# S5's state products: 64 table columns in one product, read at a stride of eight elements

## The chip, the core and the metric

The kernel runs on one core of a Trainium2 chip. The metric is the device time of one execution in microseconds. TensorE (PE) multiplies, and its weight loads (PEld) are separate instructions that overlap its products. VectorE (DVE), ScalarE (ACT) and GpSimd (POOL) work beside it. Transfers are issued from the queues of SyncE (SP) and of POOL.

## What is computed

Two decoder layers over 256 positions of width 1024, batch 1. Each layer adds half a SwiGLU, then a mixer, then half a SwiGLU, each on a normalised input. Layer 0's mixer is S5, a diagonal state-space model; layer 1's is block-sparse attention. The change is in S5 alone:

```python
def step(carry, u_c):                      # chunks of 128 positions
    bu_re = jnp.einsum('bcgn,gpn->bcgp', u_c, bb_re)
    bu_im = jnp.einsum('bcgn,gpn->bcgp', u_c, bb_im)
    pr, pi, sr, si = lax.associative_scan(combine, (lam_re_b, lam_im_b, bu_re, bu_im), axis=1)
    ...
    y = jnp.einsum('bcgp,gnp->bcgn', st_re, c_re) - jnp.einsum('bcgp,gnp->bcgn', st_im, c_im)
```

There are 64 groups of 16 channels, with 64 complex states for each group. After S5's own input product (`w_in`) come this recurrence, a GELU, a gate (`glu`) and an output product (`so`).

## The kernel before

The order of all work is written out by hand. Phases follow each other: a first SwiGLU (`f00`), S5, a SwiGLU, then layer 1. Weights stream through three raw buffers, and ACT and DVE split each into two parts (`whi` at L86 and L92, `wlo` at L87 and L93) for pairs of reduced-precision products.

**The tables.** S5's recurrence is computed in steps of four positions, with tables made on the chip from the parameters. `tables` does this during `f00`, in small pieces between the SwiGLU's products, mostly on DVE and POOL. For each of eight blocks `b` (128 channels, 8 groups) `t1_tab` (L931) turns the lag table round: DVE transposes 512 columns in 32x32 blocks (L934) into a tile `t1`, and eight transfers from POOL's queue (L940) store it in the scratch `dA[b]`. A row of `dA` is one position, group and channel of the step; its 512 columns are two halves `h` of 256. Before, each half holds eight rows `k` (real or imaginary part `i`, pair of groups `q`), with 32 states `x` side by side in each.

**The use of them.** In the S5 phase `ld_a` (L1027) loads `dA[b]` into `TA`. `t1(b)` (L1110) then multiplies: for each of 2 x 4 pairs (i, q) it makes four products, one for each quarter `a` of the 128 output partitions. The stationary operand is a run of 32 columns of `TA`, the moving operand 63 steps of the masked input `um`. The results stand in PSUM, in one bank for a block. `rot(b)` (L1124) rotates them on DVE, scans them (L1142) and rotates back on POOL (L1144 to L1147) into `hr`. `y_out(b)` (L1152) multiplies `hr` and the input `U` by two more tables, `vt` and `TB`, at L1162; there each product already fills 64 output partitions (`HALVES`). Before `t1` the input is masked in `u_masked` (L1093, `um`).

All of these products are in full precision, and each shows in the trace as two loads and two products; the names of tiles are read as result, moving operand, stationary operand.

The order in the S5 phase is the string `plan` (L1289): `tN`, `rN`, `yN`, `mN`, `vN` and `gN` are `t1`, `rot`, `y_out`, `u_masked`, `widen` and `g_tr` of block N; `w...` and `u...` are pieces of `w_in` (L1078 to L1083) and `glu` (L1203 to L1207).

```python
w256.1:2-3 t0 t1 r0 gelu w256.0:5 w256.1:4 w256.0:6 w256.1:5 w256.0:7 r1 ...
... y0 P t2 t3 r2 ... y1 m4 y2 m5 t4 r4 g1 g2 ... y3 t5 t6 ... g3 t7 y4 r7 v6 y5 ...
```

The S5 tables are stored once and loaded once; the moving operands of `w_in` are read "woven", alternating between the two halves of a piece of weights.

Of the kernel before, what the change touches and what calls it, by code (L numbers as in the profile page):

```python
# [10 lines left out]
F32 = mybir.dt.float32  # L11
# [126 lines left out]
def trunk_kernel(ctx: ExitStack, tc, x, ffn_norm, ffn_w_gate, ffn_w_up, ffn_w_down, mix_norm,  # L138
# [3 lines left out]
    nc = tc.nc  # L142
# [10 lines left out]
    def psM():  # L153
        return pp.tile([128, 512], F32, name="pM", tag="M", bufs=2)

    def psR():
        return pp.tile([128, 512], F32, name="pR", tag="R", bufs=2)

    def psA(i):
        return pp.tile([128, 512], F32, name=f"pA{i}", tag=f"A{i}", bufs=1)  # L160

    mm = nc.tensor.matmul
# [109 lines left out]
    h = [h2[:, t, :] for t in range(2)]  # L272
# [427 lines left out]
    def tables(tp):  # L700

        V, P = nc.vector, nc.gpsimd

        def T(name, *shape):
            return tp.tile([128] + list(shape), F32, name=name)
# [38 lines left out]
        ps = psR()  # L744
# [24 lines left out]
        q, y, y2, e0, e1, den = (T(n, 32) for n in ("q", "y", "y2", "e0", "e1", "den"))  # L769
# [103 lines left out]
        for i, a in enumerate((ltr, lti)):  # L873
            av = a.rearrange("p (b q) s -> p b q s", b=8)
            for k in range(2):
                P.tensor_copy(L[i][:, :, 0, k], av)
                for s in range(3):
                    o = L[i][:, :, 1, k, :, s]
# [51 lines left out]

        def t1_tab(b):  # L931

            t1 = tp.tile([128, 2, 8, 32], F32, name="t1", tag="n0", bufs=2)
            V.transpose(t1.rearrange("p s k x -> p k s x"),  # L934
                        ZC[b][1].rearrange("p i q x -> p (i q) x")[:, :, 16:80].rearrange("p k (s x) -> p k s x", s=2))
            o = dA[b].rearrange("(e f g n) (h c) -> f g h n e c", e=2, f=2, g=2, h=2)
            for a in range(4):
                for f in range(2):
                    r = 32 * a + 16 * f
                    nc.gpsimd.dma_start(o[f, a // 2, a % 2], t1[r:r + 16].rearrange("p s k x -> p s (k x)"))  # L940

        DG = {}

# [39 lines left out]
        def add_spread(b):  # L983
            work.append((0.0, B_AT, (spread, b), [(t3_tab, b), (t3_store, b - 1)] * (b % 4 == 3), 0))
            work.append((0.7, B_AT, (t1_tab, b), (), 0))
# [17 lines left out]
        while work or later or dma:  # L1003
# [4 lines left out]
            if later and later[0][0] <= now:  # L1008
                f = later.pop(0)
                f[1](*f[2:])  # L1010
                done[0] += 1
            while work and work[0][1] <= now and credit >= work[0][0] and done[0] >= work[0][4]:
                w, _, f, pe, _ = work.pop(0)
# [11 lines left out]
    LP, TA, TE, TB, TZ = [], {}, {}, {}, {}  # L1025

    def ld_a(b):  # L1027
        TA[b] = LP[0].tile([128, 512], F32, name="TA", bufs=3)
        nc.sync.dma_start(TA[b], dA[b])
# [14 lines left out]
    def s5(nxt, entry):  # L1044
        V, P = nc.vector, nc.gpsimd
        HALVES = (slice(0, 64), slice(64, 128))
# [61 lines left out]
                ld_z(b + 2)  # L1108

        def t1(b):  # L1110
            tv = TA.pop(b).rearrange("p (h i q c) -> p h i q c", h=2, i=2, c=32)
            um = UM.pop(b).rearrange("p g (q c) -> p g q c", c=64)
            ps = psA(b) if b < 4 else psM()
            for i in range(2):
                for q in range(4):
                    c = i * 256 + q * 64
                    for a in range(4):
                        mm(ps[32 * a:32 * a + 32, c + 1:c + 64], tv[:, a % 2, i, q], um[:, a // 2, q, 0:63],
                           start=True, stop=True)
            S[b] = ps  # L1120
            if b + 3 < NB:
                ld_a(b + 3)
# [125 lines left out]
        def step(word):  # L1248
# [7 lines left out]
            elif name[0] == "u":  # L1256
                glu(int(name[1]), ks)
            elif name == "x":
                if entry:
                    prep(1, 1, "s5", False)  # L1260
            elif name == "P":
                st.pump()
            elif name == "z":
                for a in VT:
                    P.memset(a, 0.0)
            elif name[0] == "a":
                if name == "a0":
                    wstack.close()
                    lstack.close()
                    XP[0] = xstack.enter_context(tc.tile_pool(name="xt2", bufs=1))  # L1270
                gate(int(name[1]))
            elif name[0] == "e":
                sigm(int(name[1]))
            elif name[0] == "o":
                b = int(name[1])
                for k in ks:
                    so(b, k // 2, k % 2)
                    if k == 3:
                        for i in range(2):
                            st.release(where["so", b], i)  # L1280
            elif name in ("gelu", "sigmoid"):
                warm(AF.Gelu_apprx_tanh if name == "gelu" else AF.Sigmoid)
            else:
                {"t": t1, "r": rot, "y": y_out, "g": g_tr, "m": u_masked, "v": widen, "k": parts}[name[0]](int(name[1]))
# [351 lines left out]
```

## Time and profile before

| | us |
|---|---|
| median of 3 runs | 909.61 |
| lowest, highest | 909.58, 911.61 |
| the profiled execution | 908.87 |
| its span, first to last instruction | 907.2 |
| TensorE busy in the span | 900.3 |
| VectorE busy in the span | 732.0 |

A matmul's end in the trace is modelled, since matmuls overlap, so the distance of starts tells more than the duration of one. The S5 phase lies at about 185 to 262 us, its tables are made between 40 and 167 us, and its state products run between 197 and 236 us.

### The profile page before, as it was taken

What the parts mean: (1) busy time and instruction counts of PE and PEld (TensorE: products, weight loads), DVE (VectorE), ACT (ScalarE), POOL (GpSimd) and SP (SyncE); (2) the same over time, 40 slices, a digit from 0 to 9 for tenths busy, and PEclk for the clock granted to TensorE, in tenths of its full rate; (3) what the DMA queues carried; (4) which work ended last, traced back from release to release, by engine and by line L of the source; (5) the groups of instructions that cost most, each with busy time, mean ns of one, the idle gap of its engine ahead of it and who ended that gap; (6) DMA issues with size and microseconds to landing.
All of it is one profiled execution on the core that took longest, in us unless ns stands there. A gap on an engine that the chain in (4) does not pass through costs nothing.

```text
span 907.2 us, 15822 instructions
## 1 busy us (share of the span) xinstructions
PE 900.3 (99%) x5874; PEld 808.9 (89%) x5874; DVE 732.0 (81%) x1272; ACT 583.5 (64%) x1115; POOL 212.7 (23%) x389
## 2 busy tenths in 40 slices
PE   9999999999999999999999999999999999999998
PEld 8888888888999999999899999998888899999997
DVE  6899999977978888777688887776898678887773
ACT  7654555567676666666576666666997576666651
POOL 6982777736702000000020000001540020000000
PEclk9999999999999999999999999999999999999999
DMA  9999788787666766655456676553554646656541
GB/s 305 255 265 331 232 281 279 243 283 247 207 193 196 239 232 220 218 189 195 143 183 218 221 233 202 200 188 106 190 173 147 224 140 233 232 188 230 186 139 47
DMA packets 143277, 191.23 MB, mean 211 GB/s; under 512 B 21128, under 2 KB 114272, under 8 KB 142944
## 3 DMA queue, kind: packets, MB, share of 16 engines
q1 hardware_dynamic: 136784, 180.38, 60.7%
q0 software_dynamic: 5696, 9.05, 3.0%
q8 instruction: 46, 0.75, 0.3%
q10 hardware_dynamic: 720, 0.80, 0.3%
q14 instruction: 31, 0.25, 0.1%
HBM read 180.15 MB, written 9.99 MB: 210 GB/s over the span
## 4 chain that ended last, share of the span: by engine, by line
PE 88%; DVE 6%; POOL 2%; issue 2%; DMA 1%; ACT 1%; DVEq 0%; ACTq 0%; POOLq 0%
PE pM L610 12%; PE pR L610 12%; PE pA L445 9%; PE pA L447 9%; PE pA L446 9%; PE pR L612 6%; PE pM L612 6%; DVE wlo L87 3%; PE pM L459 2%; PE pM L461 2%; PE pM L460 2%; PE pM L445 1%; PE pM L446 1%; PE pM L447 1%; DVE z L708 1%
## 5 line engine op out<-in xcount | busy, mean ns | idle before, releaser
L93 DVE SCALAR_TENSOR_TENSOR wlo<-raw,gT,whi 128x512 fp32r<-128x512 f32 x328 | 228.1, 748 | 41.7 <-ACT whi L92 40.7
L92 ACT ACTIVATE whi<-raw,gT 128x512 fp32r<-128x512 f32 x328 | 212.7, 709 | 3.5 <-PE pA L447 2.1
L87 DVE TENSOR_TENSOR wlo<-raw,whi 128x1024 fp32r<-128x1024 f32 x150 | 183.6, 1241 | 24.7 <-ACT whi L86 20.3
L610 PE MATMUL pM<-xa,whi 128*128 128x512 f32 x504 | 192.7, 382 | 0.0
L610 PE MATMUL pR<-xa,whi 128*128 128x512 f32 x504 | 192.5, 382 | 0.0
L86 ACT ACTIVATE whi<-raw 128x1024 fp32r<-128x1024 f32 x150 | 153.2, 1049 | 32.7 <-DMA raw<-in_ffn_w_up_dram 13.3
L612 PE MATMUL pR<-xa,wlo 128*128 128x256 f32 x504 | 137.5, 273 | 0.0
L612 PE MATMUL pM<-xa,wlo 128*128 128x256 f32 x504 | 137.5, 273 | 0.0
L445 PE MATMUL pA<-whi,ah 128*128 128x512 f32 x352 | 134.3, 382 | 0.0
L446 PE MATMUL pA<-wlo,ah 128*128 128x512 f32 x352 | 133.6, 380 | 0.0
L447 PE MATMUL pA<-whi,al 128*128 128x512 f32 x352 | 133.6, 380 | 0.0
L610 PEld LDWEIGHTS pR<-xa,whi 128*128 128x128 f32 x504 | 95.5, 189 | 13.1
L610 PEld LDWEIGHTS pM<-xa,whi 128*128 128x128 f32 x504 | 95.2, 189 | 13.1
L377 POOL TENSOR_SCALAR ms<-ss 128x1 f32<-128x1 f32 x10 | 4.1, 408 | 424.2 <-ACT sq L374 423.9
L612 PEld LDWEIGHTS pM<-xa,wlo 128*128 128x128 f32 x504 | 96.8, 192 | 1.5
L612 PEld LDWEIGHTS pR<-xa,wlo 128*128 128x128 f32 x504 | 96.9, 192 | 0.0
L642 ACT ACTIVATE sg<-gr 128x256 f32<-128x256 f32 x66 | 27.5, 417 | 75.9 <-DVE gr L635 68.5
L447 PEld LDWEIGHTS pA<-whi,al 128*128 128x128 f32 x352 | 66.7, 189 | 9.3
L445 PEld LDWEIGHTS pA<-whi,ah 128*128 128x128 f32 x352 | 66.7, 189 | 9.1
L446 PEld LDWEIGHTS pA<-wlo,ah 128*128 128x128 f32 x352 | 66.8, 190 | 7.5
L445 PE MATMUL pM<-whi,xa 128*128 128x512 f32 x160 | 62.7, 392 | 0.0
L656 ACT ACTIVATE ah<-act 128x256 fp32r<-128x256 f32 x66 | 27.4, 415 | 54.8 <-DVE act L646 54.8
(297 smaller groups left out, 1641.2 us busy)
## 6 DMA issues: line engine op xcount, KB each, us to landing
raw<-in_ffn_w_down_dram SPq DMA_DIRECT2D x44, 1024.0 KB, 5.4
raw<-in_ffn_w_gate_dram SPq DMA_DIRECT2D x80, 512.0 KB, 3.9
raw<-in_ffn_w_up_dram SPq DMA_DIRECT2D x80, 512.0 KB, 4.8
raw<-in_moba_w_qkv_dram SPq DMA_DIRECT2D x12, 1024.0 KB, 5.2
raw<-in_s_w_in_dram SPq DMA_DIRECT2D x4, 1024.0 KB, 7.3
raw<-in_s_w_glu_dram SPq DMA_DIRECT2D x4, 1024.0 KB, 7.9
raw<-in_s_w_out_dram SPq DMA_DIRECT2D x4, 1024.0 KB, 4.8
raw<-in_moba_w_out_dram SPq DMA_DIRECT2D x4, 1024.0 KB, 4.9
```

What stands on the lines that cost most here:

```text
L86: nc.scalar.activation(hi[:, c], r[:, c], AF.Copy)
L87: nc.vector.tensor_tensor(lo[:, c], r[:, c], hi[:, c].bitcast(F32), op=OP.subtract)
L92: nc.scalar.activation(hi[:, c], r[:, c], AF.Identity, scale=g)
L93: nc.vector.scalar_tensor_tensor(lo[:, c], r[:, c], g, hi[:, c].bitcast(F32), op0=OP.mult, op1=OP.subtract)
L445: mm(o, xh, wh, start=start, stop=False)
L446: mm(o, xh, wl, start=False, stop=False)
L447: mm(o, xl, wh, start=False, stop=stop)
L459: mm(o, xh, woven(wh[:, c]), start=k == 0, stop=False)
L610: mm(ps[i], a, XB[:, :, k, :].rearrange("p i (t c) -> p i c t", t=2), start=k == 0, stop=False, skip_group_check=True)
L612: mm(ps[i][:, 0:256], b, xh, start=False, stop=k == 7, skip_group_check=True)
L642: nc.scalar.activation(sg, gr[:, 0, :], AF.Silu)
L656: nc.scalar.activation(ah, a, AF.Copy)
```

## The change

Each group of four products of 32 stationary columns becomes two of 64, one for each half of the output partitions. For that the columns of a half's state must be one pattern: the table is stored with the state as the outer and the eight rows `k` as the inner index. A stationary operand is now 64 columns, eight elements apart, and the transpose at L934 writes its results eight elements apart. The stores at L940 move the same bytes in the same runs.

```diff
-            t1 = tp.tile([128, 2, 8, 32], F32, name="t1", tag="n0", bufs=2)
-            V.transpose(t1.rearrange("p s k x -> p k s x"),
+            t1 = tp.tile([128, 2, 32, 8], F32, name="t1", tag="n0", bufs=2)
+            V.transpose(t1.rearrange("p s x k -> p k s x"),
                         ZC[b][1].rearrange("p i q x -> p (i q) x")[:, :, 16:80].rearrange("p k (s x) -> p k s x", s=2))
             o = dA[b].rearrange("(e f g n) (h c) -> f g h n e c", e=2, f=2, g=2, h=2)
             for a in range(4):
                 for f in range(2):
                     r = 32 * a + 16 * f
-                    nc.gpsimd.dma_start(o[f, a // 2, a % 2], t1[r:r + 16].rearrange("p s k x -> p s (k x)"))
+                    nc.gpsimd.dma_start(o[f, a // 2, a % 2], t1[r:r + 16].rearrange("p s x k -> p s (x k)"))
...
         def t1(b):
-            tv = TA.pop(b).rearrange("p (h i q c) -> p h i q c", h=2, i=2, c=32)
+            tv = TA.pop(b).rearrange("p (c i q) -> p i q c", i=2, q=4)
             um = UM.pop(b).rearrange("p g (q c) -> p g q c", c=64)
             ps = psA(b) if b < 4 else psM()
             for i in range(2):
                 for q in range(4):
                     c = i * 256 + q * 64
-                    for a in range(4):
-                        mm(ps[32 * a:32 * a + 32, c + 1:c + 64], tv[:, a % 2, i, q], um[:, a // 2, q, 0:63],
-                           start=True, stop=True)
+                    for g, r in enumerate(HALVES):
+                        mm(ps[r, c + 1:c + 64], tv[:, i, q], um[:, g, q, 0:63], start=True, stop=True)
```

No instruction changes places; runs of products become shorter. On TensorE, at t0 and t1 between pieces of `w_in`, before (the count stands behind, output partitions by moving columns in the middle; line numbers of the changed kernel are one smaller behind L1118):

```order
L1083 MATMUL pM<-whi,xa 128x256
L1118 MATMUL pA_2426<-um,TA 32x63 x32
L1118 MATMUL pA_2461<-um,TA 32x63 x32
L1078 MATMUL pM<-whi,xa 128x256
L1079 MATMUL pM<-wlo,xa 128x256
```

The same place on TensorE in the changed kernel:

```order
L1083 MATMUL pM<-whi,xa 128x256
L1118 MATMUL pA_2426<-um,TA 64x63 x16
L1118 MATMUL pA_2445<-um,TA 64x63 x16
L1078 MATMUL pM<-whi,xa 128x256
L1079 MATMUL pM<-wlo,xa 128x256
```

Between the same neighbours, 64 products became 32. Further on TensorE, at y1, y2, t4, two transposes (g1, g2), pieces of `glu`, y3, t5 and t6, before:

```order
L1162 MATMUL pR<-hr,vt_2278 64x64 x16
L1118 MATMUL pM<-um,TA 32x63 x32
L1177 MATMUL pR<-cst,gs 128x128 x4
L1203 MATMUL pA_2935<-gf,raw 128x256 x2
L1203 MATMUL pA_2751<-gf,raw 128x256 x2
L1162 MATMUL pR<-U,TB 64x64 x8
L1162 MATMUL pR<-hr,vt_2276 64x64 x16
L1118 MATMUL pM<-um,TA 32x63 x64
```

And in the changed kernel:

```order
L1161 MATMUL pR<-hr,vt_2278 64x64 x16
L1118 MATMUL pM<-um,TA 64x63 x16
L1176 MATMUL pR<-cst,gs 128x128 x4
L1202 MATMUL pA_2855<-gf,raw 128x256 x2
L1202 MATMUL pA_2687<-gf,raw 128x256 x2
L1161 MATMUL pR<-U,TB 64x64 x8
L1161 MATMUL pR<-hr,vt_2276 64x64 x16
L1118 MATMUL pM<-um,TA 64x63 x32
```

The state products now write 64 partitions, as the output products beside them do.

## Rows read from the trace of the kernel before

**Rows 1.** The page: busy time by engine, one queue (packets, MB, share), the chain by engine

```profile
PE 900.3 (99%) x5874; PEld 808.9 (89%) x5874; DVE 732.0 (81%) x1272; ACT 583.5 (64%) x1115; POOL 212.7 (23%) x389
...
q8 instruction: 46, 0.75, 0.3%
...
PE 88%; DVE 6%; POOL 2%; issue 2%; DMA 1%; ACT 1%; DVEq 0%; ACTq 0%; POOLq 0%
```

**Rows 2.** Waits of PE, whole kernel: us in total, times, longest

```profile
PE pM L1078 <- issue: 1.2, 1, 1.2
PE pR L1526 <- POOL ones L252: 1.1, 1, 1.1
PE pR L546 <- DVE act L533: 0.2, 1, 0.2
```

**Rows 3.** Windows: stretch, its length, busy us by engine, then clock, DMA

```profile
core 0: us, PE busy (x) PEld busy (x) DVE busy (x) ACT busy (x) POOL busy (x), PEclk, DMA share, GB/s
100.00:120.00 20.00, 19.77 (x96) 17.00 (x95) 19.89 (x27) 9.37 (x16) 13.06 (x23) 1.00 0.85 274
120.00:140.00 20.00, 20.00 (x155) 17.29 (x154) 17.92 (x27) 11.23 (x18) 15.19 (x26) 1.00 0.89 274
140.00:160.00 20.00, 20.00 (x97) 17.50 (x96) 19.57 (x41) 11.14 (x18) 16.06 (x30) 1.00 0.81 261
197.00:255.00 58.00, 56.76 (x1141) 52.17 (x1140) 49.17 (x81) 41.26 (x87) 33.13 (x32) 1.00 0.73 253
```

**Rows 4.** The chain, 199 to 232 us: start, us, piece, records

```profile
201.39 1.24 issue
...
211.59 1.90 PE pA L1118 x128
...
220.38 2.95 PE pR L1162 x96
223.33 1.02 PE pM L1118 x64
...
226.67 1.55 PE pR L1162 x48
```

**Rows 5.** The chain, 86 to 117 us: the transposes in it

```profile
88.21 0.62 DVE t L934
...
97.67 0.70 DVE t L934
...
106.88 0.10 DVE t L934
```

**Rows 6.** PE in order of time, 116 to 117 us; the bracket is idle time before

```profile
116.67 0.44 PE L546 MATMUL pR<-cst,act 128*128 128x128 f32 x2 [0.23 <-DVE act L533]
```

**Rows 7.** DMA queues, 199.9 to 201.3 us: packets, MB, share of 16 engines

```profile
q1 hardware_dynamic: 271, 0.55, 101.1%
q8 instruction: 1, 0.02, 4.4%
```

**Rows 8.** All engines in order of time, 220 to 224.5 us: start, us

```profile
221.00 0.73 POOL L1147 TENSOR_TENSOR hr<-pv,pv 128x256 f32<-128x256 f32 x1
...
222.23 1.10 PE L1162 MATMUL pR<-hr,vt 128*64 128x64 f32 x32
222.26 0.90 ACT L1100 ACTIVATE um<-U,gm 128x256 f32<-128x256 f32 x2
...
223.26 1.09 PE L1118 MATMUL pM<-um,TA 128*32 128x63 f32 x64
```

**Rows 9.** Four lines on DVE: count, ns least/median/most, first and last start

```profile
L934 DVE STREAM_TRANSPOSE t<-ze x8: 694/700/711, 88.1 to 157.6; 128x512 f32<-128x512 f32 x8
...
L899 DVE STREAM_TRANSPOSE cb<-cn x2: 1036/1052/1069, 73.9 to 74.9; 128x512 f32<-128x512 f32 x2
...
L1168 DVE STREAM_TRANSPOSE gs<-yg x8: 422/445/446, 212.1 to 249.9; 128x256 f32<-128x256 f32 x8
...
L301 DVE COPY perm<-cst x1: 273/273/273, 1.6 to 1.6; 128x128 f32<-128x128 f32 x1
```

**Rows 10.** Weight loads in order of time, 21.7 to 22.6 us

```profile
21.97 0.41 PEld L1544 LDWEIGHTS pR<-rn,perm 128*128 128x128 f32 x2
22.29 0.19 PEld L445 LDWEIGHTS pM<-whi,xa 128*128 128x128 f32 x1
```

**Rows 11.** PE in order of time, 200.5 to 200.9 us

```profile
200.56 0.28 PE L1078 MATMUL pM<-whi,xa 128*128 128x256 f32 x1
200.67 0.27 PE L1079 MATMUL pM<-wlo,xa 128*128 128x256 f32 x1
```

**Rows 12.** L1162's weight loads: count, ns least/median/most

```profile
L1162 PEld LDWEIGHTS pR<-hr,vt x256: 137/138/139, 210.4 to 248.9; 128*64 128x64 f32 x128
```

## Prediction

> **What bounds the kernel now.** I read the page first. TensorE has work for 900.3 of the 907.2 us, and the chain of work that ended last runs through it for 88% [rows 1]. The waits of TensorE say how much of the span it lost: three waits are listed in the whole kernel, 1.2 us for "issue" before L1078, 1.1 us at the start, and 0.2 us for VectorE's `act` before L546 [rows 2]. So a change in TensorE's own time passes to the end almost one for one, wherever it stands after the last of these waits. The state products (`t1`, L1118) stand in 197 to 255 us; there TensorE idles 1.24 of 58 us at full granted clock [rows 3], and all of that is the one "issue" piece of the chain at 201.39 [rows 4]. Before 117 us the picture is another one: VectorE is busy for 19.89 of 20 us between 100 and 120 us [rows 3], the chain runs through it [rows 5], and the 0.23 us wait at 116.67 is where TensorE takes the chain over [rows 6]. The change touches both stretches: the products, and the VectorE transposes that prepare their table (L934).
>
> **The products themselves.** Each product shows as two records, each a weight load and a stream. A block had 32 products (64 records), now 16 (32 records). The chain has 1.90 us for two blocks and 1.02 us for one [rows 4], so a block adds 0.88 us: 13.75 ns a record, or 55 ns for each set of four column groups that run side by side. The output products (`y_out`, L1162) already have the new shape, 64 weight columns in each half: 2.95 us for 96 records and 1.55 us for 48 [rows 4], so 48 records add 1.40 us, 29.2 ns a record, 58.3 ns for the pair of halves. By that row a new block takes 32 x 29.2 = 933 ns against 880, 53 ns more, and eight blocks 0.4 us more. They stream 64 columns and the state products 63, so the other end is the old pace of 55 ns, which adds nothing. I take +0.4, the row of the same shape. Halving the instructions therefore does not halve the time: four narrow products ran side by side where two wide ones will.
>
> **Where runs meet.** What is left of a run after its records, 1.02 - 0.88 = 0.14 us after `t1` and 1.55 - 1.40 = 0.15 us after `y_out` [rows 4], is the passage to the next kind of product. Two `y_out` blocks in a row pay it once. In four places a `y_out` and a `t1` follow each other (y0 to t2, y2 to t4, y3 to t5, t7 to y4). Once both use halves, these could go as quietly as y1 to y2: 4 x 0.15 = 0.6 us saved. The other end is 0, if the passage belongs to the change of tables and not to that of shape. I take -0.6, because y1 to y2 changes tables too.
>
> **The stall behind t0 and t1.** At 201.39 TensorE waits 1.24 us and nothing in the profile holds it [rows 4]. The instruction queue q8 moved 46 packets and 0.75 MB [rows 1]: 16 KB each. TensorE's records are 2 x 5874, so that queue fits TensorE's program at 64 bytes an instruction, 256 to a packet (an estimate from these two rows). One such packet was moved between 199.9 and 201.3 us, while the data queue filled the DMA engines (101% with the overlap counted) [rows 7]. t0 and t1 together are 128 records of each kind, 256 instructions, used up in 1.9 us, a whole packet. My reading is that the burst emptied the fetched instructions before the next packet came. After the change the burst is 128 instructions in about the same time, and the next 128 belong to products of 0.11 us and more, so the packet has some 7 us longer (64 products x 0.11). I take the stall as gone: -1.24 us, with 0 as the other end, if it is no matter of fetching.
>
> Not all of it reaches the end. y2's second part starts at 222.23, and the `hr` that it reads is finished by POOL at 221.00 + 0.73 = 221.73; t4 starts at 223.26, and ACT finishes its `um` at 222.26 + 0.90 = 223.16 [rows 8]. The chain of the rotation (DVE, then POOL) begins after t2 and will move forward, but ACT's copy and masks ahead of it are back to back and move less. I put what y2 and t4 then wait at +0.3 us (bounds: 0, and the whole 1.24).
>
> **The transposes.** L934 still transposes 512 columns eight times, but writes at a stride of eight elements. It takes 700 ns now; L899, the same operation writing at a stride of sixteen in runs of four, takes 1052 [rows 9]. The copy at L301 reads at a stride of four in runs of 32 and needs 273 ns for 128 elements; two unstrided transposes, 445 ns for 256 elements (L1168) and 700 for 512, make 1.0 ns an element and 190 fixed, 318 for 128 [rows 9]. So that stride costs nothing, and L899's price may be that of its short runs. The runs will be 64 long: I side with L301 and take 0; the upper end is 0.35 us each. Three of the eight are in the chain before TensorE takes it over, at 88.21, 97.67 and 106.88 [rows 5]; there VectorE's time is the kernel's, and the upper end is 3 x 0.35 = +1.05 us. The other five lie where VectorE works ahead of TensorE: VectorE idles 2.1 us from 120 to 140 and 0.4 us from 140 to 160 [rows 3], and what it falls behind it can make up before TensorE catches up with it, so I take 0 for them too (upper end 5 x 0.35 = 1.75 us). The stores to `dA` (L940) and the loads of `TA` keep their number, sizes and order; every row still moves as one run of 256 elements.
>
> **The load at a stride.** No row of the trace shows a weight load whose columns lie apart, and this is the term that decides. A full load of 128 columns can be had in 0.10 us: the two loads of L1544 span 0.41 us with 0.19 for each, so the second began at 22.19, and the next began at 22.29 [rows 10]. 64 columns are thus 50 ns, just inside the 58 ns of a pair: there is hardly any slack, where 32 columns (25 ns) left half of the 55 free. For a free stride speaks the moving side: the products of `w_in` read it in an order that alternates between elements 128 apart, and still stream 256 columns in 0.11 us [rows 11]. For a price speaks VectorE's L899 above, 1052 against 700. I take 0 in the sum; it is the nearest in engine. The upper end is a load of double length, 100 ns: 42 ns more for each of 16 pairs in 8 blocks, 128 x 42 = +5.3 us. A gain below 0 is excluded: the stream alone already takes the 55 ns of the old pace.
>
> [...]
>
> **Sum.** +0.4 - 0.6 - 1.24 + 0.3 + 0 + 0 = -1.1 us. The profiled execution took 908.87 us (span 907.2 and 1.67 around it), which gives 907.8; the runs' median is 909.61, 0.74 above it, so I forecast 908.5 us for the median.
>
> **Rivals.** First, *the strided load is slow*: at double length the products take 5.3 us on top of the 0.4; the stall and the passages still save 1.24 + 0.6, less 0.3: 909.6 + 5.3 + 0.4 - 1.5 = 913.8 us, slower. The place is the 128 pairs of L1118. With the other terms at -1.1 it passes 0.3% (2.7 us) from 3.8 us on, 30 ns a pair, which is 88 ns for 64 columns or 1.8 times today's; VectorE's ratio 1052 / 700 is 1.5. Second, *the gain does not arrive*: the stall at 201.39 stays or turns up behind the denser t7, y4, y5 (64 + 96 + 96 records, 4 us), or y2 and t4 wait it out; with the transposes at their upper price this is 909.6 + 0.4 - 0.6 + 1.05 = 910.5 us, no change. That is also the case in which the change does not do what its smaller number of instructions suggests. Third, *more is gained than the rows hold*: the only idle time in reach is 1.24 + 0.6 + 0.23 us, which gives 907.5 at best; for 0.3% something the trace does not show would have to be freed, say 906 us.
>
> **How the numbers follow.** A measurement of this kernel tells a change from none at about 0.3%, 2.7 us. Forecast 0.52, second rival 0.17, slow load 0.26 (some of it milder than double, two in a hundred much worse because the halves' loads no longer overlap), more gained 0.05. So faster 0.05, same 0.70 (with the mildest of the slow loads), slower 0.25. The range needs the slow load inside: from 907.5, all terms at their good ends, to 914.8, the first rival with the transposes at their upper price.
>
> **What would show it.** In the profile after: L1118's 256 records at 28 to 30 ns apart, about 0.93 us a block and 1.9 for t0 and t1 together; the "issue" piece near 201 us gone; L934 at 700 ns. If t0 and t1 take 3 us or more and the loads of L1118 stand well above the 138 ns of L1162's [rows 12], the slow load is right and the forecast wrong. If the products are as told and the end has not moved, the waits before L1162 and L1118 show where the gain went.

## The result, and the profile after

The changed kernel takes 917.18 us, the median of six runs (917.06 to 917.98); the kernel before, on the same chip, 909.93 (six runs, 909.58 to 911.61). The ratio is 1.0079, with a 95% interval from 1.0066 to 1.0092: the change costs 7.3 us. The forecast was 908.5 with a range up to 914.8; the time lies above the range.

The profiled execution took 917.06 us, with a span of 915.3, 8.1 us more than before. The page of the changed kernel, to be held against [rows 1]:

```profile
PE 908.9 (99%) x5618; PEld 816.3 (89%) x5618; DVE 736.0 (80%) x1272; ACT 583.9 (64%) x1115; POOL 215.8 (24%) x389
...
q8 instruction: 44, 0.72, 0.3%
...
PE 97%; DVE 1%; issue 0%; ACT 0%; DVEq 0%; POOL 0%; ACTq 0%; POOLq 0%
```

TensorE has 256 records fewer (64 in each of t0 to t7 became 32) and works 8.6 us longer: it is not waiting more, it is slower at less. The chain now runs through it for 97%, but that share says little: two profiles of one and the same kernel below, the one with a stride of two, have 88% and 97%. Its waits in the changed kernel, against [rows 2]:

```profile
PE pR L546 <- DVE act L533: 1.2, 2, 0.9
PE pR L1525 <- POOL ones L252: 1.1, 1, 1.1
```

The 1.2 us of "issue" are gone, and VectorE's wait before L546 has grown from 0.2 to 1.2. The lines of the change itself in the changed kernel: weight loads of the state products and of the output products beside them ([rows 12] has the latter before), and the transposes (against [rows 9]); count, ns least/median/most, first and last start:

```profile
L1118 PEld LDWEIGHTS pA<-um,TA x128: 195/218/228, 199.0 to 217.4; 128*64 128x64 f32 x128
L1161 PEld LDWEIGHTS pR<-hr,vt x256: 138/138/139, 212.8 to 257.1; 128*64 128x64 f32 x128
L934 DVE STREAM_TRANSPOSE t<-ze x8: 1096/1110/1125, 88.5 to 159.5; 128x512 f32<-128x512 f32 x8
```

The two loads have the same size. The one with its columns side by side shows 138 ns, the strided one 218. The transpose went from 700 to 1110 ns. The chain of the changed kernel, 195 to 245 us, against [rows 4]:

```profile
199.09 4.07 PE pA L1118 x58
...
213.94 3.86 PE pA L1118 x64
...
227.64 2.02 PE pM L1118 x32
...
233.53 3.86 PE pM L1118 x64
...
241.73 2.09 PE pM L1118 x27
243.82 2.80 PE pR L1161 x83
```

(Some records are missing from the chain, which is why a piece reads x58 or x27; the times are those of whole pieces.) The five pieces of the state products sum to 15.90 us; before they were 1.90, 1.90, 1.02, 1.90 and 1.02, together 7.74. A further block (3.86 - 2.02) costs 1.84 us, 115 ns for a pair of halves, where 0.93 us was forecast. At the other end of the table TensorE takes the chain over later, against [rows 6]:

```profile
118.14 0.44 PE L546 MATMUL pR<-cst,act 128*128 128x128 f32 x2 [0.93 <-DVE act L533]
```

So the 8.1 us of span are: products +8.16 (15.90 - 7.74), the stall -1.24, the later takeover +1.47 (118.14 - 116.67), y4 and y5 -0.15 (2.80 after t7, 2.95 where another kind of product stands ahead). That makes +8.2. The medians differ by less, 7.3, because the profiled execution of the kernel before was a quick one (908.87 us against a median of 909.93) with an early takeover: two kernels below with the same transposes have it at 117.21 and 117.49 instead of 116.67.

### The profile page after: what moved, and what is told of

Read it like the earlier page. It is cut to its first block, busy times and chain, and to the rows that moved or that the text cites. A ratio compares the mean times of both kernels' runs of the same rounds, so it can differ in the third digit from the quotient of the medians.

```text
span 915.3 us, 15310 instructions
## 1 busy us (share of the span) xinstructions
PE 908.9 (99%) x5618; PEld 816.3 (89%) x5618; DVE 736.0 (80%) x1272; ACT 583.9 (64%) x1115; POOL 215.8 (24%) x389
## 4 chain that ended last, share of the span: by engine, by line
PE 97%; DVE 1%; issue 0%; ACT 0%; DVEq 0%; POOL 0%; ACTq 0%; POOLq 0%
PE pR L610 12%; PE pM L610 12%; PE pA L445 10%; PE pA L446 10%; PE pA L447 10%; PE pM L612 6%; PE pR L612 6%; PE pM L445 3%; PE pM L446 3%; PE pM L447 3%; PE pM L459 2%; PE pM L461 2%; PE pM L460 2%; PE pR L1161 1%; PE pA L520 1%; PE pR L362 1%
```

## The experiments

Two causes were on the table: the read of the table at a stride (products) and the write of it at a stride (transposes). The experiments take them apart, then ask what it is in the read that costs, and whether the reading of the stall was right. The ratios below are each against the kernel before on the same chip, with 95% intervals.

### The two halves of the change, each alone

**The read alone.** The change's products on a table transposed and stored as before:

```diff
-            t1 = tp.tile([128, 2, 32, 8], F32, name="t1", tag="n0", bufs=2)
-            V.transpose(t1.rearrange("p s x k -> p k s x"),
+            t1 = tp.tile([128, 2, 8, 32], F32, name="t1", tag="n0", bufs=2)
+            V.transpose(t1.rearrange("p s k x -> p k s x"),
...
-                    nc.gpsimd.dma_start(o[f, a // 2, a % 2], t1[r:r + 16].rearrange("p s x k -> p s (x k)"))
+                    nc.gpsimd.dma_start(o[f, a // 2, a % 2], t1[r:r + 16].rearrange("p s k x -> p s (k x)"))
```

> The change's products, which read the table at a stride of eight elements, on a table that is transposed and stored as before: the states and rows of the table stand in another order than the products take them, so this kernel computes something else; its time is that of the read alone. If the products carry the whole of the loss, the chain has them at 4.07, 3.86, 2.02, 3.86 and 2.09 us as in the changed kernel, L934 is back at 700 ns, TensorE takes the chain over at 116.7 to 117.2 instead of 118.1, and the median is the changed kernel's less what the transposes cost. If they cost 1.2 (three of 0.41 in the chain) that is 916.0; if VectorE makes up for it, 917.2. Under 914 another cause than the two would be at work.

Measured: 916.46 us against 910.32, ratio 1.0068 [1.0055, 1.0081], +6.1 us. The lines of that kernel:

```profile
L934 DVE STREAM_TRANSPOSE t<-ze x8: 694/698/711, 88.9 to 158.4; 128x512 f32<-128x512 f32 x8
...
L1118 PEld LDWEIGHTS pA<-um,TA x128: 195/218/228, 198.4 to 216.8; 128*64 128x64 f32 x128
...
213.29 3.86 PE pA L1118 x64
...
227.00 2.03 PE pM L1118 x32
...
117.49 0.44 PE L546 MATMUL pR<-cst,act 128*128 128x128 f32 x2 [0.54 <-DVE act L533]
```

The transpose is back at 698 ns, the load stays at 218, and the products are as dear as in the changed kernel (4.07, 3.86, 2.03, 3.89 and 2.09 in the chain, two of them shown). TensorE takes the chain over at 117.49, a little behind the 117.2 that I had put as the latest.

**The write alone.** The same edit the other way round, on the kernel before: the table written at a stride of eight, read in runs of 32.

> The other half alone: the table is transposed and stored as in the changed kernel (written at a stride of eight elements), and read as before, in runs of 32 columns, four products to a pair (i, q); it computes something else, as the reading no longer fits the table. L934 takes 1110 ns, the products and the stall at 201 us are those of the kernel before (1.90 for two blocks, 1.24 of issue). If the three transposes in the chain pass to the end, TensorE takes the chain over about 1.2 us later than in the kernel before, and the median is 911.1; if VectorE makes up for it, 909.9, no difference. The two halves' gains and losses should then add up to the change's 7.3 us.

Measured: 911.43 us against 910.32, ratio 1.0014 [1.0004, 1.0024], +1.1 us. Waits of TensorE, the transposes and the takeover in that kernel:

```profile
PE pM L1078 <- issue: 1.2, 1, 1.2
PE pR L1162 <- issue: 0.4, 1, 0.4
...
L934 DVE STREAM_TRANSPOSE t<-ze x8: 1106/1114/1132, 88.8 to 159.7; 128x512 f32<-128x512 f32 x8
...
118.45 0.44 PE L546 MATMUL pR<-cst,act 128*128 128x128 f32 x2 [0.92 <-DVE act L533]
```

The stall at t0 and t1 is there again with the old products, and a second one of 0.4 us before L1162 that the kernel before doesn't have. The two halves add up: 6.1 + 1.1 = 7.2, and the whole change cost 7.3. The read is the larger part by far.

### Is it the stride, or the shape of 64 columns?

**Columns side by side.** The change's two products for a pair, but the 64 columns of a stationary operand adjacent. For that the transposes and stores are those of before, and the load of the table puts the rows of both halves side by side:

```diff
-        nc.sync.dma_start(TA[b], dA[b])
+        for hf in range(2):
+            nc.sync.dma_start(TA[b].rearrange("p (m h x) -> p h m x", h=2, m=8)[:, hf],
+                              dA[b].rearrange("p (h m x) -> p h m x", h=2, m=8)[:, hf])
...
-            tv = TA.pop(b).rearrange("p (c i q) -> p i q c", i=2, q=4)
+            tv = TA.pop(b).rearrange("p (i q c) -> p i q c", i=2, q=4)
```

> Kernel: two products of 64 columns as in the change, but the 64 columns lie side by side. The tile t1, its transpose and its stores are those of before; the table is put in order while it is loaded into TA, by two transfers (one for each half) with runs of 32 elements. Theory 'stride': what is slow in the changed kernel is the load of weights eight elements apart (57.5 ns a record, 218 ns a load). Then here the records of L1118 stand 28 to 30 ns apart, the loads read 138 ns, t0 and t1 together take 1.9 us, L934 reads 700 ns, the issue stall of 1.24 us behind t0 and t1 is gone, and the time is 908 to 909.5 us, 0 to 1.5 below before. Rival 'shape': two halves of 64 columns of this table are slow in themselves (the loads of the two halves come one after the other); then the records stay at 57 ns, t0 and t1 take 4 us, and the time is 913 to 916 us. If the shorter runs of the loads of TA are late, L1118 waits for a DMA, which the waits of PE would name.

Measured: 915.04 us against 910.42, ratio 1.0053 [1.0040, 1.0066]. By its time alone the stride would not be the cause. The trace shows that the time goes elsewhere. Weight loads of the products and two pieces of the chain in that kernel, then waits of TensorE, another piece of the chain, and the table's transfers (count, KB each, median us from issue to landing):

```profile
L1120 PEld LDWEIGHTS pM<-um,TA x128: 132/138/138, 228.1 to 240.2; 128*64 128x64 f32 x128
228.31 1.02 PE pM L1120 x31
...
233.19 1.86 PE pM L1120 x64
...
PE pA L1120 <- DMA TA<-dA: 2.1, 1, 2.1
PE pA L1120 <- ACT um L1102: 1.2, 1, 1.2
...
204.69 10.90 DMA TA<-dA
...
TA<-dA SPq DMA_DIRECT2D x16, 128.0 KB, 5.0
```

The loads are at 138 ns and a further block costs 1.86 - 1.02 = 0.84 us: the shape is cheap, the stride is not. What the kernel loses it loses while it waits, mostly for transfers. Those of the table move runs of 32 elements, land in 5.0 us for half a table each (before: 4.1 for a whole one), and TensorE waits 2.1 us for a table and 1.2 for an `um`. (ACT made that `um` late because it had waited 3.1 us for weights of `glu`; that the short runs delayed these too is not shown.) Behind the idle time TensorE is slower too, as the windows of that kernel show (granted clock in the third column from the right):

```profile
212.00:217.00 5.00, 2.75 (x62) 2.50 (x64) 3.94 (x6) 3.46 (x9) 0.00 (x0) 0.91 0.83 119
217.00:219.00 2.00, 2.00 (x13) 1.51 (x10) 1.80 (x4) 0.00 (x0) 0.00 (x0) 0.50 0.93 277
219.00:222.00 3.00, 3.00 (x15) 2.68 (x15) 2.73 (x6) 2.51 (x6) 2.00 (x2) 0.91 1.18 271
```

After 2.25 us of idle time in five, the granted clock is 0.50 while TensorE is busy throughout: products of 512 columns start 0.43 us apart there (217.93 and 218.36) and 0.22 us apart from 219.58 on. This one stretch shows that the lower clock follows the idle time, not that the idle time causes it.

**Stride kept, quarters kept.** The change's table at a stride of eight, but read by four products of 32 columns as before:

```diff
+            tv = TA.pop(b).rearrange("p (h c i q) -> p h i q c", h=2, i=2, q=4)
...
-                    for g, r in enumerate(HALVES):
+                    for a in range(4):
...
```

> Kernel: the changed table (state outer, eight rows inner, transpose written at a stride of eight, columns read at a stride of eight), but the four products of 32 columns of before. Theory 'stride, loads of different column groups overlap': 32 columns apart take about 32 x 1.8 = 57 ns, against the 55 ns that four records stream, so the records go from 13.8 to about 15 ns, t0 and t1 take 2.0 us, the stall behind them stays, and only the transposes cost: L934 at 1110 ns, TensorE takes over the chain 1.2 to 1.5 us later, time 911 to 912 us. Rival 'strided loads come one after the other': 128 columns at 0.9 ns are 115 ns for four records, 29 a record, t0 and t1 take 3.9 us, time 916 to 918 us.

Measured: 912.41 us, ratio 1.0021 [1.0012, 1.0030], just above what was expected if loads of several column groups overlap, and far from the 916 to 918 of loads one after the other. Loads and chain in that kernel:

```profile
L1118 PEld LDWEIGHTS pA<-um,TA x256: 137/151/165, 199.6 to 216.2; 128*32 128x32 f32 x128
...
203.78 1.55 issue
...
214.29 2.22 PE pA L1118 x125
...
226.36 1.20 PE pM L1118 x62
```

At the same stride a block costs 1.02 us instead of 1.84 (64 ns for a set of four, 55 before; 115 for a pair of 64). Four short loads side by side cost much less than two long ones at the same stride. With 256 instructions in t0 and t1 the stall is there again.

**Which strides are dear.** The same 64 columns, with 2 or 4 of the eight rows `k` interleaved, so that the columns lie two or four elements apart (for 4, `m=2`, `l=4` and `k=4`):

```diff
+            t1 = tp.tile([128, 2, 4, 32, 2], F32, name="t1", tag="n0", bufs=2)
+            V.transpose(t1.rearrange("p s h x k -> p h k s x"),
+                        ... .rearrange("p (h k) (s x) -> p h k s x", s=2, k=2))
...
+        for hf in range(2):
+            nc.sync.dma_start(TA[b].rearrange("p (m h x) -> p h m x", h=2, m=4)[:, hf],
+                              dA[b].rearrange("p (h m x) -> p h m x", h=2, m=4)[:, hf])
...
+            tv = TA.pop(b).rearrange("p (m c l) -> p m l c", l=2, c=64)
...
```

Two elements, one execution (it took 908.59 us):

> Kernel: two products of 64 columns that lie two elements (8 bytes) apart; the transpose writes at a stride of two, and the table is loaded into TA in runs of 64 elements. [...] If the price grows with the distance, loads and L934 stand between the side-by-side case and the stride of eight (138 and 218 ns; 700 and 1110 ns).

The same kernel again, timed eleven times:

> Kernel: columns two elements apart again, timed. Theory: products as cheap as side by side (0.9 us a block), the stall of 1.24 us gone, 0.1 us less at each meeting of y_out and t1, against 0.15 us more for each transpose, of which some 0.8 us reach TensorE at 117 us: 0.9 to 1.5 us faster than before, 908.5 to 909.5 us. If what the single look showed was chance, it is the time of before, 909.5 to 910.5 us.

Four elements, one execution:

> Kernel: the same with a stride of four elements (16 bytes), runs of 128 elements in the load of TA. [...]

Measured: 908.91 us at two against 910.44 (ratio 0.9986 [0.9977, 0.9995], by the ratio 1.3 us faster than before: the best version here) and 918.22 at four (910.42 before). Loads and transposes of the kernel at two, then at four, there with two pieces of the chain:

```profile
L1121 PEld LDWEIGHTS pA<-um,TA x128: 136/138/140, 198.4 to 212.9; 128*64 128x64 f32 x128
L934 DVE STREAM_TRANSPOSE t<-ze x8: 796/854/867, 88.6 to 158.5; 128x512 f32<-128x512 f32 x8
```

```profile
L1121 PEld LDWEIGHTS pA<-um,TA x128: 193/217/217, 200.4 to 218.7; 128*64 128x64 f32 x128
L934 DVE STREAM_TRANSPOSE t<-ze x8: 1450/1540/1608, 88.9 to 161.8; 128x512 f32<-128x512 f32 x8
...
215.21 3.83 PE pA L1121 x64
...
228.88 2.00 PE pM L1121 x32
```

| columns apart, elements | load, ns | a further block, us | transpose L934, ns | TensorE takes over at, us |
|---|---|---|---|---|
| 1 | 138 | 0.84 | 699 | 116.67, 117.21, 117.49 |
| 2 | 138 | 0.85 | 854 | 117.47, 117.49, 117.76 |
| 4 | 217 | 1.83 | 1540 | 119.48 |
| 8 | 218 | 1.84 | 1110 | 118.14, 118.44, 118.45, 118.74 |

(A further block is the chain's piece for two less that for one. Of these edits only those of the transposes lie ahead of the takeover, so kernels with the same L934 stand together in it; they still differ among themselves by up to 0.8 us.) The load has a step between two elements and four (138 and 217 ns), and none between one and two (138 both) or between four and eight (217 and 218): its price does not grow with the distance. Three elements were not run, and what sets the step these rows do not show.

The transposes behave otherwise: stride four is dearer than eight, and its pattern has one dimension more. The last column shows how they pass to the end. Against the mean at one element (117.12), TensorE takes over 0.45, 2.36 and 1.32 us later at strides two, four and eight; three transposes in the chain, at (854 - 699), (1540 - 699) and (1110 - 699) ns each, make 0.47, 2.52 and 1.23. The first of these is smaller than the spread of the takeover at one element, the other two are not.

### How long is one load, and do two overlap?

**One half after the other.** The change, with all products of one half of the channels ahead of the other's, so that no load stands beside a load of the other half:

```diff
-            for i in range(2):
-                for q in range(4):
-                    c = i * 256 + q * 64
-                    for g, r in enumerate(HALVES):
+            for g, r in enumerate(HALVES):
+                for i in range(2):
+                    for q in range(4):
+                        c = i * 256 + q * 64
```

> Kernel: the changed kernel with its products in another order: the eight of one half of the output partitions first, then the eight of the other, where the change alternates halves. Theory 'one strided load takes about 115 ns, and the loads of the two halves overlap': products that follow each other in one half cannot hide their loads behind each other, so the records go from 57.5 to about 115 ns, t0 and t1 from 4.1 to about 7.5 us, and the time rises by some 14 us, to 930 us. Rival 'one strided load takes 57 ns, and all loads come one after the other': the order changes nothing, records 57.5 ns, time 917 us.

As a control the same edit on the version with a stride of two:

> The version with a stride of two elements, with all products of one half of the channels ahead of all of the other, so that no load overlaps the load of the other half; a control for the same order at a stride of eight, where a further block cost 3.00 us, 94 ns a record. If those 94 ns are the strided load, this order is cheaper here: 50 to 58 ns a record, by the two unstrided full loads of L1544 (0.10 us for 128 columns), so 1.6 to 1.9 us a further block and two blocks at 3.4 to 4.0 us. If the 94 ns are what products of one half cost one after another whatever they load, a further block is 3.00 us here too.

Measured: 927.89 and 914.37 us, one execution each (the kernel before has 910.44 and 909.17 on their chips). The chain at a stride of eight:

```profile
216.74 6.42 PE pA L1118 x64
...
233.01 3.42 PE pM L1118 x32
```

and at two:

```profile
212.93 3.28 PE pA L1121 x64
...
226.05 1.73 PE pM L1121 x32
```

A further block is 6.42 - 3.42 = 3.00 us, 94 ns for each of its 32 records, against 3.28 - 1.73 = 1.55 us, 48 ns. At a stride of eight neither expectation is met: 94 lies between 57 and 115. For these products the stride is all that differs, so 46 ns are its price for one load. I read 48 and 94 as the loads themselves, since the loads of L1544, whose products stream only two columns, give 50 ns for 64 columns as well (0.10 us for 128) [rows 10]; a strided load is then about twice as long. With the halves alternating a pair takes 53 ns at a stride of two (0.85 / 16) and 115 at eight (1.84 / 16): in the first case the two loads hide each other almost whole (5 ns over one load), in the second a fifth of a load is left over (21 ns). Why the overlap is less complete there is open.

### Was the stall a late packet of instructions?

**Moving the packets.** The kernel before with 32 small products put in during `f00`; nothing reads their results, and by the estimate of 256 instructions to a packet they shift which later instructions share one:

```diff
+                        ps = psR()
+                        for _ in range(32):
+                            mm(ps[0:32, 0:4], ones[:, 0:32], ones[:, 0:4], start=True, stop=True)
```

> Kernel: before, with 32 products of 32 by 4 columns of ones into scratch added in the fifth step of the first SwiGLU, which nothing reads: 128 more instructions on TensorE, far ahead of S5. Theory 'the 1.24 us stall behind t0 and t1 is a late packet of instructions': which instructions a packet of 256 ends with has shifted by half a packet, so the stall at L1078 behind t0 and t1 is gone or stands elsewhere, though t0 and t1 still take 1.9 us. Rival 'TensorE waits there for something that t0 and t1 cause': the stall of 1.2 us stays at the same product. The time is within 2 us of before either way; what counts is the list of TensorE's waits.

Measured: 914.88 us, 2.4 us more than the upper end of what I had expected. The small products, which I had thought half hidden, stand on TensorE for 2.19 us, and further on it waits 1.7 us for an `um` that ACT made late, having waited 2.5 us for weights of `glu`:

```profile
86.99 2.19 PE L573 MATMUL pR<-ones 128*32 128x4 f32 x64
```

Two of TensorE's waits in that kernel, the chain around t5 and t6 (`t1`'s products are L1122 there), and the instruction queue from 233 to 234.4 us (packets, MB, share of the engines):

```profile
PE pA L1122 <- ACT um L1104: 1.7, 1, 1.7
PE pM L1122 <- issue: 1.2, 1, 1.2
...
232.77 1.66 PE pM L1122 x106
234.43 1.17 issue
235.60 0.53 PE pM L1122 x22
...
q8 instruction: 1, 0.02, 4.8%
```

The stall before L1078 has gone, though t0 and t1 still run through in 1.9 us; no packet of q8 shows there from 199 to 203 us. One of the same length stands some 30 us later, in the middle of t5 and t6, between products of one line that wait for nothing the trace shows, and one packet of q8 moved in that stretch, as one did at the old place [rows 7]. What the edit changes for `t0` to `t7` is the place of their instructions in the program. Over all twelve profiles the wait for "issue" goes with the count: it is listed in the four with 256 TensorE instructions in two blocks (46 packets on q8: the kernel before, the write alone, the quarters, this one) and in none of the eight with 128 (44 packets). Those four hold five such stalls, two of them in the write alone, and in each TensorE goes on 2.3 to 2.6 us after a packet of q8 is recorded: packets at 200.2 (the kernel before), 202.8 (the quarters), 202.1 and 237.6 (the write alone) and 233.0 us (this kernel), TensorE on again at 202.63, 205.33, 204.41, 240.10 and 235.60. What a packet holds the trace does not say, so the late packet is the reading that fits all of this, not one that was seen.

## Why the prediction was wrong

**The load at a stride** is the step that failed: "I take 0 in the sum; it is the nearest in engine", argued from `w_in`'s moving operand [rows 11]. That operand streams 256 columns in 0.11 us, read alternately 128 elements apart; a weight load of 64 columns takes 94 ns with them eight apart, 48 with two: the row came from the right engine and the wrong operation. Its own sign for that came: t0 and t1 took 4.07 us, and the loads show 218 ns beside 138. The first rival had the mechanism and its place, the 128 pairs, and almost the length of a load: 100 ns against 94 measured. It had the price too small because it let the two loads of a pair hide each other whole, 100 ns for a pair, 42 more than without the stride. The pair takes 115: 128 x 15 = 1.9 us more than its 5.3.

**The transposes** were taken as 0, because L301's copy reads at a stride for nothing [rows 9]. A copy that reads does not tell what a transpose that writes costs; L899, the same operation, did (1052 against 1110). The step's upper end, 0.35 us each and 1.05 in the chain, is just below what came, 0.41 and about 1.2, and the write alone cost 1.1 us in the time. That the five later transposes would cost nothing was right: behind the takeover VectorE appears in no wait of TensorE in the changed kernel.

With these two put right the first rival gives 913.8 + 1.9 + 1.2 = 916.9; measured were 917.2. That it closes so well is partly luck. In the changed kernel the five pieces hold 8 x 1.84 us and 1.18 more, where the kernel before has 8 x 0.88 and 0.70 more: with y4's 0.15 the passages cost 0.3 where the rival lets them save 0.6, and its wait of 0.3 did not come. So the rival's terms make 7.3 and the pieces of the two traces 8.2; they meet because the traces have a quick execution of the kernel before, and the medians do not.

**The products** of the new shape: +0.4 from y_out's row, 0.93 us a block. The version with a stride of two has that shape without the slow load, and there a further block takes 0.85 us, less than the 0.88 of before: the pace of the pair, 53 ns, is even below the 55 that the prediction took as its floor. Still its five pieces sum to 8.09 us against 7.74, +0.35: what is dearer is the first block of each run.

**The meetings** of `y_out` and `t1` were to save 0.6. In the version with a stride of two:

```profile
198.44 2.07 PE pA L1121 x64
...
211.30 1.92 PE pA L1121 x64
...
223.06 1.07 PE pM L1121 x32
...
235.38 2.80 PE pR L1165 x96
```

Held against that kernel's own other passages, they do: t2 and t3 behind y0 take 0.15 us less than t0 and t1 behind `w_in`, t5 and t6 the same 1.92, t4 0.04 less than t7 (1.07, 1.11), y4 behind t7 2.80 against 2.95, together 0.5 us. Held against the kernel before, only y4 saves anything: t2 and t3 took 1.90 there, t4 1.02. So products and meetings together came to +0.35 - 0.15 = +0.2 where the sum has +0.4 - 0.6 = -0.2, and how the 0.2 is to be split between them is a matter of what one compares with.

**The stall** went, -1.24, and the run with 32 products put in, where a stall of the same length stands at 234.43 us instead of 201.39, fits the reading of its cause. Of the second rival, that it would turn up behind the denser t7, y4 and y5, nothing came; in the write alone, with the old products, a stall of 0.4 us did turn up at that place. (The 64 + 96 + 96 in that rival are instructions, loads and products together, not records.)

**y2 and t4** were to wait 0.3 us. They do not, and in the version with a stride of two, where the products are as short as forecast, no such wait is listed either. The term was unneeded.

So with a free load the sum comes out near as a whole, -1.1 us forecast and -1.3 measured at a stride of two (by the interval -2.1 to -0.5), but partly by luck: the products and meetings came 0.4 dearer than forecast, the wait of 0.3 did not come, and the transposes of that version cost some 0.45 that the sum doesn't have. What is left open between them, 0.65 us, is less than the interval leaves open (0.8 either way), and kernels with the same transposes differ by up to 0.8 us in their takeover (116.67 to 117.49). The change failed by one property of its table: columns eight elements apart, where two would have done.

## What to carry to other kernels

Price an operand's pattern by a row of the same operation; a row of another operand of the same engine misled here, and so did a copy's row for a transpose. When a stationary operand has to be interleaved, keep its fp32 columns at most two elements apart (138 ns a load here, against 217 at four). And when two loads are to hide each other, price the pair, not the load: here two loads of 48 ns took 53, two of 94 took 115.

## What was not expected of the hardware

- Products of one half that follow each other, each with a weight load of 64 fp32 columns, stand 48 ns apart with the columns two elements apart and 94 with eight. Strides of one and two show the same record of 138 ns, four and eight the same 217 to 218: a step, no slope.
- A transpose of 512 columns in 32x32 blocks on VectorE takes 699, 854, 1540 and 1110 ns when it writes at strides of one, two, four and eight elements. Why four is the dearest is open (its pattern and that of two have one more dimension).
- TensorE can stop for 1.2 us in the middle of a run of equal products with nothing in the trace that holds it, and the place moves by some 30 us when 32 products are put in at 87 us. Late instructions are the reading that fits, not one that a trace shows; each such stall ends 2.3 to 2.6 us after a packet of q8.
